# Cross-attention products on 32-row and 32-column tiles in a hybrid decoder layer

## The chip, the core and the metric

The kernel runs on one core of one Trainium2 chip. The metric is device time of one execution in microseconds (us), lower is better. Three executions of the kernel before took 487.26, 488.16 and 488.65 us; the median is 488.16 us.

## What is computed

One decoder layer with five branches that read the same input `x` (256 tokens, 1024 features): A and B are attentions with masks, C a forgetting attention, D a gated delta rule, E a cross-attention into 256 memory tokens. Each branch gives 384 features per token, which are gated by `silu(z)`, multiplied by the branch's output matrix and by a sigmoid of merge logits, and summed. An output matrix, a residual and a LayerNorm follow. The change is in branch E alone, four heads of 96 features:

```
k, v = split(mem_n @ w_kv, 2)
q = q.reshape(B, S, 4, 96) * 96 ** -0.5
p = softmax(einsum('bshd,bmhd->bhsm', q, k))
o_e = einsum('bhsm,bmhd->bshd', p, v).reshape(B, S, 384)
...
o = o * silu(z)
y = einsum('bsnc,ncd->bsnd', o, w_branch)
y = sum(sigmoid(merge_logits) * y, axis=2)
```

## The kernel before

All large products are made from float32 operands that are split in two parts, `hi` (ACT, L123) and `lo` (DVE, L124), and multiplied three times (`mm3`, L128: hi·hi, hi·lo, lo·hi). They are cut into units: a unit loads 128x1024 (or 128x384) weights by DMA, splits them, and multiplies them in two or three chunks. The list `ORDER` says in which order the units come; its end is `ze eq mk mv merge_d merge_b merge_e`. A `merge_x` block has eight pairs of units: 24 products of merge logits (`mm<-xhi,hi` and so on) and 9 products of the gated branch output with its output matrix (`mm<-f,hi`). Splits run one unit ahead (`SA`), in three buffers (`NHI`).

Everything small runs as side streams, Python generators of which up to three advance by one step after each chunk: attention of C, A and B (`attend`), the delta rule, the memory LayerNorm, and `cross`, which is branch E. Where a unit needs the output of a stream (`need("oge")` in `merge_e`), the streams are driven on until it is there. On top of that the framework's scheduler orders the instructions of each engine, so a line that is written next to another one need not run next to it. Each engine then takes its own instructions strictly in that order.

The matrices of PSUM are tiles of four kinds: three `mm` (the large products), one `lg` of two banks (logits), two `tp` (transposes), one `av` (values).

Branch E before: `evac_k` (L853) and `evac_ve` (L863) take keys and values out of PSUM. A head's 96 features lie across the three 128-row tiles of keys and queries, so `HQ` (L880) cuts the heads into one or two pieces of rows, six products for four heads. The last head is multiplied over all 128 rows, against a copy of the keys (`kp`) whose first 32 rows are zero. `cross` (L882) runs four chains, one for 128 tokens and two heads, two chains alive at a time (`LIVES[3]`): logits (L897), maximum on DVE (L900), exponential on ACT (L905), four transposes (L911), copy (L914), value products with tokens as rows (L920). After the second pair of heads the values are scaled by the reciprocal of the sums (L925). Then `token_gate` (L870) transposes the result back to features as rows (L875), multiplies it by the gate and splits it.

A product of two float32 operands that are not split (L897, L920, L135) leaves two records in the trace, that is two passes. A transpose leaves one.

Of the kernel before, what the change touches and what calls it, by code (L numbers as in the profile page):

```python
# [10 lines left out]
F32R = mybir.dt.float32r  # L11
AF = mybir.ActivationFunctionType
ALU = mybir.AluOpType
AX = mybir.AxisListType

P = 128
S = 256
D = 1024
KD = 8
BW = 384  # L20
H = 6
HD = 64
NB = 5
# [7 lines left out]
         " merge_c zb bq2 ze eq mk mv merge_d merge_b merge_e").split()  # L31
MERGES = [n for n in ORDER if n.startswith("merge")]
STREAMS = "base c levels solve b a gate_d cross norm".split()
LIVES = 2, 2, 1, 2

# [40 lines left out]
def kernel(ctx: ExitStack, tc: tile.TileContext, T: dict, out: bass.AP):  # L76
# [19 lines left out]
    def f3t(dt=F32, shape=(P, 3, S)):  # L96
        return f3.tile(list(shape), dt, tag="f3", name=nm("f3"))

    def spt(tag, shape, dt=F32, bufs=None):
        return sp.tile(list(shape), dt, tag=tag, name=nm(tag), bufs=bufs)  # L100
# [47 lines left out]
    R = {}  # L148
# [99 lines left out]
    def stepper(gens, n, force=False):  # L248


        k = 0
        for g in list(gens):
            if k == n:
                break
            if not force and ready.get(id(g), 0) > tick[0]:
                continue
            try:
                d = next(g)
                if d is not False:
# [593 lines left out]
    def evac_k(p, m, b):  # L853
        if m == 0:
            R["ke"] = f3t()
        A_.activation(R["ke"][:, m], p, AF.Copy)
        if m == 2:
            kp = R["kp"] = spt("kp", (P, S), bufs=1)
            V_.memset(kp[0:32], 0.0)
            V_.tensor_copy(kp[32:64], p[32:64])  # L860
            V_.tensor_copy(kp[64:128], p[64:128])

    def evac_ve(p, t):  # L863
        if t == 0:
# [5 lines left out]
    def token_gate(o, zs, br, scalar=None):  # L870
        dst = R["og" + br] = (f3t(F32R), f3t(F32R))
        for m in range(3):
            pt = tpps((P, S))
            for t in range(2):
                PE.transpose(pt[:, t * P:(t + 1) * P], o[:, t, m * P:(m + 1) * P], ident)  # L875
            yield
            yield from gate(pt, zs, m, dst, scalar)
        flag("og" + br)

    HQ = [[(0, 0, 96)], [(0, 96, 128), (1, 0, 64)], [(1, 64, 128), (2, 0, 32)], [(2, 0, 128)]]  # L880

    def cross():  # L882
        yield from wait("ze", "eq", "ve")
        ke, kp, qe, ve = R["ke"], R["kp"], R["eq"], R["ve"]
        oe = f3t(shape=(P, 2, BW))
        avt, smt = {}, {}

        def pair(t, g):
            if g == 0:
                smt[t] = spt("sme", (P, 4), bufs=2)  # L890
            lg = lgps()
            hs = (2 * g, 2 * g + 1)
            for x, h in enumerate(hs):
                parts = HQ[h]
                for i, (m, a0, a1) in enumerate(parts):
                    krhs = kp if (h == 3) else ke[:, m]
                    PE.matmul(lg[:, x, :S], qe[a0:a1, m, t * P:(t + 1) * P], krhs[a0:a1], start=i == 0, stop=i == len(parts) - 1)  # L897
            yield
            mxe = spt("mxe", (P, 2), bufs=3)
            V_.tensor_reduce(mxe, lg[:, :, :S], axis=AX.X, op=ALU.max, negate=True)  # L900
            yield
            pes = []
            for x, h in enumerate(hs):
                pe = spt("pr", (P, S), bufs=NPR)
                A_.activation(pe, lg[:, x, :S], AF.Exp, bias=mxe[:, x:x + 1], accum_out=smt[t][:, h:h + 1])  # L905
                pes.append(pe)
            yield
            p2 = tpps((P, 2, 2, P))
            for pe, pt in zip(pes, (p2[:, 0], p2[:, 1])):
                for x in range(2):  # L910
                    PE.transpose(pt[:, x], pe[:, x * P:(x + 1) * P], ident)  # L911
            yield
            pT = spt("pT", (P, 2, 2, P), bufs=2)
            A_.activation(pT, p2, AF.Copy)  # L914
            yield
            if g == 0:
                avt[t] = avps((P, 4, 96))
            for i, h in enumerate(hs):
                for x in range(2):
                    PE.matmul(avt[t][:, h], pT[:, i, x], ve[:, x, h * 96:(h + 1) * 96], start=x == 0, stop=x == 1)  # L920
            if g == 1:
                yield
                rse = spt("rse", (P, 4), bufs=2)
                V_.reciprocal(rse, smt[t])
                V_.tensor_tensor(oe[:, t].rearrange("p (h d) -> p h d", h=4), avt[t],  # L925
                                 rse[:, :, None].to_broadcast([P, 4, 96]), op=ALU.mult)

        todo = [pair(t, g) for t in range(2) for g in range(2)]
        live = []
        while todo or live:  # L930
            while todo and len(live) < LIVES[3]:
                live.append(todo.pop(0))
            stepper(live, LIVES[3])
            yield 1
        yield from token_gate(oe, R["ze"], "e")

    def d_gate():
        yield from wait("od", "zd")
# [176 lines left out]
def _layout(inp):  # L1115

    f = np.float32
    x = np.asarray(inp["x"], f)[0]
    w = np.asarray(inp["w_in"], f)[0]
    b = np.asarray(inp["b_in"], f)[0]  # L1120
    kv = np.asarray(inp["w_mem_kv"], f)[0]
    offs = np.cumsum([0, 1152, 2304, 384, 1152, 6, 1152, 6, 6, 384, 1920, 5120])
    oA, oBqk, oBv, oC, oCf, oD, oBeta, oDec, oE, oZ, oM = offs[:11]
    start = {"aq": oA, "ak": oA + 384, "av": oA + 768, "cq": oC, "ck": oC + 384, "cv": oC + 768,
             "dq": oD, "dk": oD + 384, "dv": oD + 768, "eq": oE, "bv": oBv}
    for g in range(3):
        start[f"bq{g}"] = oBqk + 384 * g
        start[f"bk{g}"] = oBqk + 1152 + 384 * g
    for n, i in BR.items():
        start["z" + n] = oZ + 384 * i  # L1130

    def cols(name):
        if name == "mk":
            return kv[:, 0:384]
        if name == "mv":
            return kv[:, 384:768]
        return w[:, start[name]:start[name] + 384]

    def fm(m):
        n = m.shape[1] // P  # L1140
        return m.reshape(KD, P, n, P).transpose(1, 2, 0, 3).reshape(P, n * 1024)

    r = {}
    r["xT"] = x.T.reshape(KD, P, S).transpose(1, 0, 2)
    r["x"] = x
    r["mem"] = np.asarray(inp["mem"], f)[0]
    r["wf"] = np.stack([fm(cols(n)) for n in FM])
    r["wt"] = np.stack([cols(n).reshape(KD, P, 384).transpose(1, 0, 2).reshape(P, 3072) for n in TM])
    wm = np.stack([fm(w[:, oM + 1024 * n:oM + 1024 * (n + 1)]) for n in range(NB)]).reshape(NB, P, KD, 1024)
    wb = np.asarray(inp["w_branch"], f)[0].reshape(NB, 3, P, KD, P).transpose(0, 2, 3, 1, 4).reshape(NB, P, KD, 384)  # L1150
    r["wm"], r["wb"] = wm.reshape(NB, P, KD * 1024), wb.reshape(NB, P, KD * 384)
    cs = [slice(start["cv"], start["cv"] + 384), slice(oCf, oCf + 6), slice(oDec, oDec + 6), slice(oBeta, oBeta + 6)]
    r["wcs"] = np.concatenate([w[:, s] for s in cs], 1).reshape(KD, P, 402).transpose(1, 0, 2).reshape(P, KD * 402)
    r["vcb"] = np.concatenate([b[s] for s in cs])[None]
    bc = [np.zeros(384, f) if n == "mk" else b[start[n]:start[n] + 384] for n in FM] + [b[oM:oM + 5120]]
    r["bcol"] = np.concatenate(bc).reshape(-1, P).T
    r["vb"] = np.stack([b[start[n]:start[n] + 384] for n in ("av", "bv")])[None]
    r["wo"] = np.asarray(inp["w_out"], f)[0].reshape(KD, P, D).transpose(1, 0, 2).reshape(P, 8192)
    r["convw"] = np.asarray(inp["conv_w"], f)[0].reshape(4, 9, P).transpose(2, 1, 0)
    r["adt"] = np.concatenate([np.asarray(inp["a_log"], f)[0], np.asarray(inp["dt_bias"], f)[0]])[None]  # L1160
    r["gnw"] = np.concatenate([np.asarray(inp["gdn_norm_w"], f)[0]] * 2)[:, None]
    r["mgb"] = np.stack([np.asarray(inp["mem_ln_g"], f).reshape(KD, P).T, np.asarray(inp["mem_ln_b"], f).reshape(KD, P).T], 1)
    r["lngb"] = np.stack([np.asarray(inp["ln_g"], f)[0], np.asarray(inp["ln_b"], f)[0]])[None]
    r["cst"] = _consts()
    return {k: np.ascontiguousarray(v) for k, v in r.items()}
# [16 lines left out]
```

## Time and profile before

| | |
|---|---|
| median of 3 runs | 488.16 us |
| profiled execution | 489.4 us |
| its span, first to last instruction | 487.6 us |
| mean granted clock of TensorE | 0.977 |
| PE busy | 469.8 us, 96% of the span |
| DVE busy | 336.1 us, 69% |
| ACT busy | 270.6 us, 55% |
| HBM read | 79.37 MB |

The table's span lies 1.8 us below the time of the same execution: the rest is before the first and after the last instruction. A matmul's recorded length contains its way through the array, so two that follow each other overlap in the record. What one costs on PE is therefore read from the distance between the starts of neighbours. "[0.89 <-ACT hi L123]" behind a row says that the engine was idle for 0.89 us and which result ended it.

### The profile page before, as it was taken

How to read it: one execution, taken by the hardware profiler on the slowest of the kernel's cores; microseconds unless marked ns; L12 is line 12 of the kernel's file. 1: busy time of each engine (PE TensorE's matmuls, PEld its weight loads, DVE VectorE, ACT ScalarE, POOL GpSimd, SP SyncE). 2: the span in 40 equal slices, each digit the busy share in tenths (PEclk: the TensorE clock that was granted, in tenths of full speed). 3: DMA queues.
4: the chain of work that ended last, by engine and by line, in shares of the span. 5: the costliest groups of instructions: out<-in, count | busy, mean ns of one | idle time of the engine just before them, and what ended most of it. 6: DMA issues, size and time to landing. Idle time of an engine off the chain costs nothing.

```text
span 487.6 us, 10147 instructions
## 1 busy us (share of the span) xinstructions
PE 469.8 (96%) x3957; PEld 439.2 (90%) x3957; DVE 336.1 (69%) x764; ACT 270.6 (55%) x521; POOL 30.5 (6%) x36
## 2 busy tenths in 40 slices
PE   7999999989989999999999999999999999999994
PEld 3999999979988999999999999988987899999973
DVE  4898998875983435568976665666667457678747
ACT  5546684763773333466854455846657445566610
POOL 0000040120000000000001210000012111100000
PEclk9999999989998699999999999999999999999997
DMA  8995667554444113245656786252753345577302
GB/s 263 367 369 169 202 202 250 161 144 121 146 105 116 44 60 114 84 140 174 204 155 209 222 260 215 78 167 77 279 191 120 104 125 173 182 231 235 131 1 86
DMA packets 35050, 81.38 MB, mean 167 GB/s; under 512 B 8969, under 2 KB 17467, under 8 KB 34875
## 3 DMA queue, kind: packets, MB, share of 16 engines
q1 hardware_dynamic: 34715, 80.22, 52.1%
q8 instruction: 31, 0.51, 0.4%
q10 hardware_dynamic: 288, 0.52, 0.3%
q14 instruction: 16, 0.13, 0.1%
HBM read 79.37 MB, written 1.36 MB: 166 GB/s over the span
## 4 chain that ended last, share of the span: by engine, by line
PE 84%; DVE 6%; DMA 4%; ACT 3%; issue 1%; SPq 1%; POOL 0%; DVEq 0%; POOLq 0%
PE mm L128 67%; PE lg L135 3%; PE lg L128 2%; DVE lo L124 2%; PE tp L128 2%; ACT pr L754 2%; PE av L135 2%; PE lg L897 1%; PE lg L773 1%; DMA raw<-in_wcs_dram 1%; ACT hi L123 1%; DVE pr L738 1%; DMA scr<-t 1%; PE av L920 1%; PE tp L632 1%
## 5 line engine op out<-in xcount | busy, mean ns | idle before, releaser
L124 DVE TENSOR_TENSOR lo<-raw,hi 128x1024 fp32r<-128x1024 f32 (+4 forms) x163 | 170.7, 1049 | 89.6 <-ACT hi L123 89.0
L128 PE MATMUL mm<-xhi,hi 128*128 128x256 f32 x776 | 221.3, 285 | 0.4 <-ACT hi L123 0.4
L123 ACT ACTIVATE hi<-raw 128x1024 fp32r<-128x1024 f32 (+4 forms) x163 | 146.4, 901 | 131.8 <-PE mm L128 90.2
L128 PE MATMUL mm<-xhi,lo 128*128 128x256 f32 x776 | 219.2, 283 | 0.3 <-DVE lo L124 0.3
L128 PE MATMUL mm<-xlo,hi 128*128 128x256 f32 x776 | 219.0, 282 | 0.0
L128 PEld LDWEIGHTS mm<-xhi,hi 128*128 128x128 f32 x776 | 148.1, 191 | 3.9 <-issue 2.0
L128 PEld LDWEIGHTS mm<-xhi,lo 128*128 128x128 f32 x776 | 147.9, 191 | 3.4 <-issue 1.6
L128 PEld LDWEIGHTS mm<-xlo,hi 128*128 128x128 f32 x776 | 148.2, 191 | 0.9 <-issue 0.7
L128 PE MATMUL mm<-f,hi 128*128 128x256 f32 x240 | 45.3, 283 | 0.4 <-ACT hi L123 0.4
L972 POOL TENSOR_TENSOR yacc<-yacc,yt 128x256 f32<-128x256 f32 x24 | 19.8, 824 | 303.3 <-DVE yt L971 294.1
L128 PEld LDWEIGHTS mm<-f,hi 128*128 128x128 f32 x240 | 36.7, 188 | 0.9 <-ACT hi L123 0.6
L128 PE MATMUL mm<-f,lo 128*128 128x256 f32 x120 | 33.9, 283 | 0.0
L128 PEld LDWEIGHTS mm<-f,lo 128*128 128x128 f32 x120 | 22.6, 188 | 0.1
L754 ACT ACTIVATE pr<-pr,mm 128x128 f32<-128x128 f32 (+1 forms) x36 | 15.9, 444 | 4.8 <-DVE mm L745 4.8
L954 ACT ACTIVATE th<-mm,bcol 128x256 f32<-128x256 f32 x40 | 18.4, 460 | 0.0
L128 PE MATMUL mm<-hi,xhi 128*128 128x384 f32 (+1 forms) x48 | 15.8, 353 | 2.0 <-ACT hi L123 2.0
L128 PE MATMUL mm<-lo,xhi 128*128 128x384 f32 (+1 forms) x48 | 16.8, 349 | 0.4 <-DVE lo L124 0.4
L135 PE MATMUL lg<-f,f 64*128 64x256 f32 (+1 forms) x144 | 16.9, 351 | 0.0
L738 DVE CUSTOM_DVE_ANT_0 pr<-lg,cst 128x128 f32<-128x128 f32 (+1 forms) x48 | 14.4, 352 | 3.6 <-PE lg L135 3.6
L971 DVE SCALAR_TENSOR_TENSOR yt<-th,mm 128x256 f32<-128x256 f32 x32 | 13.5, 420 | 4.7 <-PE mm L128 2.9
L128 PE MATMUL mm<-hi,xlo 128*128 128x384 f32 (+1 forms) x48 | 16.5, 345 | 0.0
L480 POOL TENSOR_SCALAR_AFFINE_SELECT pr<-pr 128x256 f32<-128x256 f32 x6 | 9.5, 1591 | 93.9 <-DVE pr L479 93.9
(234 smaller groups left out, 570.6 us busy)
## 6 DMA issues: line engine op xcount, KB each, us to landing
raw<-in_wf_dram SPq DMA_DIRECT2D x60, 512.0 KB, 4.5
raw<-in_wm_dram SPq DMA_DIRECT2D x40, 512.0 KB, 3.6
raw<-in_wb_dram SPq DMA_DIRECT2D x40, 192.0 KB, 2.4
raw<-in_wt_dram SPq DMA_DIRECT2D x12, 384.0 KB, 3.6
raw<-in_wo_dram SPq DMA_DIRECT2D x8, 512.0 KB, 5.9
gr<-gscr SPq DMA_DIRECT2D x12, 128.0 KB, 3.6
raw<-in_wcs_dram SPq DMA_DIRECT2D x3, 402.0 KB, 6.3
raw<-in_mem_dram SPq DMA_DIRECT2D x2, 512.0 KB, 3.2
```

The source lines that it names most:

```text
L123: A_.activation(hi, src, AF.Copy)
L124: V_.tensor_tensor(lo, src, hi.bitcast(F32), op=ALU.subtract)
L128: ins = PE.matmul(pt, l, r, start=start, stop=stop)
L135: PE.matmul(pt, l, r, start=start, stop=stop)
L480: G_.affine_select(E[:, 0::2], E[:, 0::2], pattern=[[0, 2], [1, P]], compare_op=ALU.is_ge, fill=-BIG, base=0, channel_multiplier=-1)
L632: PE.matmul(pt[r, x], Uc[r, 6 * t + h], V[r, t, h], start=True, stop=True)
L738: V_.tensor_tensor_reduce(l[:, sl], pts[x][:, sl], mk[x][:, sl], 1.0, 3.0e38, ALU.add, ALU.min, mx[x][:, t, g:g + 1])
L754: A_.activation(l[:, sl], l[:, sl], AF.Exp, bias=mms[x][:, t:t + 1], scale=-1.0, accum_out=sm_[x][:, t, g:g + 1])
L773: PE.transpose(lg[:, x, i * P:(i + 1) * P], L[x][0][:, i * P:(i + 1) * P], ident)
L954: A_.activation(th, p, AF.Tanh, bias=bcol[:, i:i + 1], scale=0.5)
L971: V_.scalar_tensor_tensor(yt, st_["th"], 1.0, st_["p"], op0=ALU.add, op1=ALU.mult)
L972: (V_ if last else G_).tensor_tensor(yacc[:, d], yacc[:, d], yt, op=ALU.add)
```

## The change

The columns of E's query, key and gate weights (and the rows of its output matrix) are permuted on the host, so that head `h` has rows 32h to 32h+31 of each of the three tiles. The masked copy `kp` is gone. `cross` runs one chain for 128 tokens and all four heads; the second chain starts when the first has made its transposes. `cross` now also waits for `ogb`, the end of branch B's attention.

```diff
-        if m == 2:
-            kp = R["kp"] = spt("kp", (P, S), bufs=1)
-            V_.memset(kp[0:32], 0.0)
-            V_.tensor_copy(kp[32:64], p[32:64])
-            V_.tensor_copy(kp[64:128], p[64:128])
...
     def cross():
-        yield from wait("ze", "eq", "ve")
+        yield from wait("ze", "eq", "ve", "ogb")
...
+        HE = [slice(32 * h, 32 * h + 32) for h in range(4)]
+        def tokens(t):
+            ts = slice(t * P, (t + 1) * P)
             lg = lgps()
-            for x, h in enumerate(hs):
-                for i, (m, a0, a1) in enumerate(HQ[h]):
-                    PE.matmul(lg[:, x, :S], qe[a0:a1, m, ts], krhs[a0:a1], ...)
+            pts = [lg[:, 0, :S], lg[:, 1, :S], tpps((P, S)), tpps((P, S))]
+            for m in range(3):
+                together(*[(pts[h], qe[r, m, ts], ke[r, m], m == 0, m == 2) for h, r in enumerate(HE)])
...
+            V_.reciprocal(rse, sme)
+            for h in range(4):
+                V_.tensor_scalar(pes[h], pes[h], rse[:, h:h + 1], None, op0=ALU.mult)
...
-                    PE.matmul(avt[t][:, h], pT[:, i, x], ve[:, x, h * 96:(h + 1) * 96], ...)
+            av = avps((P, 3, P))
+            for m in range(3):
+                for x in range(2):
+                    together(*[(av[r, m], ve[:, x, 96 * h + 32 * m:96 * h + 32 * m + 32], pTs[h // 2][:, h % 2, x], x == 0, x == 1)
+                               for h, r in enumerate(HE)])
+            V_.tensor_tensor(g, av, zs[:, :, ts], op=ALU.mult)
+            split(dst[0][:, :, ts], dst[1][:, :, ts], g)
...
-        yield from token_gate(oe, R["ze"], "e")
```

`together` (L132) issues its products one behind the other and nothing more. The logits are now 24 products of 32 rows, the values 48 products of 32 columns; the six transposes back and the scaling of the values are gone, and the probabilities are scaled instead, eight times.

How the instructions stand: first PE inside the block `mv`, before its last unit (`mm<-hi,big` are products of the memory, `f` the queries and keys of E, `lg_4426` the transposes of branch B). Before:

```order
L128 MATMUL mm_4453<-hi_4475,big_3186 128x384
L128 MATMUL mm_4453<-lo_4476,big_3186 128x384
L128 MATMUL mm_4453<-hi_4475,big_3187 128x384
L128 MATMUL mm_4452<-hi_4510,big_3186 128x384
L128 MATMUL mm_4453<-hi_4510,big_3186 128x384
L773 MATMUL lg_4426<-cst,pr_4245 128x128 x3
```

Now:

```order
L128 MATMUL mm_4449<-lo_4472,big_3186 128x384
L128 MATMUL mm_4449<-hi_4471,big_3187 128x384
L135 MATMUL tp_4776<-f_734_4347,f_705_4199 128x256
L135 MATMUL tp_4775<-f_734_4347,f_705_4199 128x256
L135 MATMUL tp_4776<-f_734_4347,f_705_4199 128x256
L128 MATMUL mm_4448<-hi_4506,big_3186 128x384
L128 MATMUL mm_4449<-hi_4506,big_3186 128x384
L773 MATMUL lg_4426<-cst,pr_4245 128x128 x3
```

Three of the first chain's logit products, of heads 2 and 3, stand directly ahead of the last unit of `mv`, and three more (`tp_4775`, `tp_4776`, `tp_4775`) stand ten products earlier; the two other heads (`lg_4774`, six products) follow much later, behind the last pair of B.

Second, PE in `merge_d`, from the unit that follows B's last twelve exponentials on. Before (B's exponentials are not shown, they are ACT's):

```order
L128 MATMUL mm_4984<-f_470_2951,hi_4935 128x256
L128 MATMUL mm_4984<-f_469_2950,lo_4936 128x256
L911 MATMUL tp_4660<-cst,pr_4631 128x128 x2
L897 MATMUL lg_4599<-f_734_4347,f_705_4199 128x256 x2
L897 MATMUL lg_4599<-kp_4442,f_705_4199 128x256
L911 MATMUL tp_4660<-cst,pr_4633 128x128 x2
L128 MATMUL mm_5040<-f_469_2950,hi_5001 128x256
L128 MATMUL mm_5040<-f_470_2951,hi_5001 128x256
L128 MATMUL mm_5005<-xhi,lo_4981 128x256
```

Now:

```order
L128 MATMUL mm_4961<-f_470_2951,hi_4865 128x256
L128 MATMUL mm_4961<-f_469_2950,lo_4866 128x256
L773 MATMUL lg_4682<-cst,pr_4501 128x128 x3
L128 MATMUL mm_5039<-f_469_2950,hi_4982 128x256
L128 MATMUL mm_5039<-f_470_2951,hi_4982 128x256
L128 MATMUL mm_4986<-xhi,lo_4958 128x256
```

E's products and transposes have left this place, and the three that stood 18 products ahead of it (`lg_4595`, L897) too. B's own six transposes (L773), which came later before, stand here instead.

Third, PE in `merge_d` at the second chain of E (all of it new):

```order
L128 MATMUL mm_5143<-xlo,hi_5120 128x256
L135 MATMUL tp_4902<-f_734_4347,f_705_4199 128x256 x3
L128 MATMUL mm_5143<-xhi,lo_5121 128x256
L128 MATMUL mm_5143<-xhi,hi_5120 128x256
L135 MATMUL tp_4903<-f_734_4347,f_705_4199 128x256 x3
L909 MATMUL lg_4879<-cst,pr_4823 128x128 x2
...
L135 MATMUL av_4922<-pT_4897,f_778_4568 32x128 x2
L128 MATMUL mm_5176<-f_470_2951,hi_5139 128x256
L135 MATMUL lg_4901<-f_734_4347,f_705_4199 128x256 x6
L135 MATMUL av_4922<-pT_4899,f_778_4568 32x128 x2
L135 MATMUL av_4922<-pT_4897,f_778_4568 32x128 x2
```

Head 2 and head 3 of the second chain stand alone, three products each, with large products between them; heads 0 and 1 (`lg_4901`) come later, in the middle of the first chain's values. The values are written in the order of the heads, two products first, then 22 in one row.

## Rows read from the trace of the kernel before

**Rows 1.** The page: busy us of each engine, share of the span, instructions.

```profile
PE 469.8 (96%) x3957; PEld 439.2 (90%) x3957; DVE 336.1 (69%) x764; ACT 270.6 (55%) x521; POOL 30.5 (6%) x36
```

**Rows 2.** Groups by line: shapes xcount | busy us, mean ns | idle before.

```profile
L897 PE MATMUL lg<-f,f 32*128 32x256 f32 (+2 forms) x20 | 6.4, 419 | 0.0
...
L897 PE MATMUL lg<-kp,f 128*128 128x256 f32 x4 | 1.4, 431 | 0.0
...
L920 PE MATMUL av<-f,pT 128*128 128x96 f32 x32 | 4.1, 271 | 0.0
...
L767 DVE TENSOR_SCALAR pr<-pr,rs 128x128 f32<-128x128 f32 (+1 forms) x36 | 10.2, 327 | 0.2
```

**Rows 3.** Timeline of PE, one logit block: start us, length, instruction [idle before].

```profile
364.49 0.28 PE L128 MATMUL mm<-xhi,lo 128*128 128x256 f32 x1
364.61 1.85 PE L897 MATMUL lg<-f,f 96*128 96x256 f32 x6
...
366.60 0.29 PE L128 MATMUL mm<-xlo,hi 128*128 128x256 f32 x1
...
364.82 0.38 PE L897 MATMUL lg<-f,f 96*128 96x256 f32 x1
```

**Rows 4.** Timeline of PE, one block of value products.

```profile
376.49 0.28 PE L128 MATMUL mm<-f,hi 128*128 128x256 f32 x1
376.61 1.03 PE L920 MATMUL av<-f,pT 128*128 128x96 f32 x8
...
377.62 0.28 PE L128 MATMUL mm<-f,lo 128*128 128x256 f32 x1
```

**Rows 5.** Timeline of PE, one pair of transposes.

```profile
403.46 0.28 PE L128 MATMUL mm<-xhi,hi 128*128 128x256 f32 x1
403.58 0.38 PE L875 MATMUL tp<-cst,f 128*128 128x128 f32 x2
...
403.91 0.28 PE L128 MATMUL mm<-xhi,lo 128*128 128x256 f32 x1
```

**Rows 6.** Timeline of PE, branch B's logits: two heads, 64 rows each.

```profile
332.16 0.28 PE L128 MATMUL mm<-big,lo 128*128 128x256 f32 x1
332.37 0.93 PE L135 MATMUL lg<-f,f 64*128 64x128 f32 x8
...
333.56 0.28 PE L128 MATMUL mm<-big,lo 128*128 128x256 f32 x1
```

**Rows 7.** Timeline of PE, branch B's values: two heads, 64 columns each.

```profile
386.60 0.28 PE L128 MATMUL mm<-xlo,hi 128*128 128x256 f32 x1
386.80 0.87 PE L135 MATMUL av<-pT,f 128*64 128x256 f32 x8
...
387.83 0.28 PE L128 MATMUL mm<-xhi,hi 128*128 128x256 f32 x1
```

**Rows 8.** Timeline of PE, ahead of the last unit of `mv`.

```profile
340.11 0.34 PE L128 MATMUL mm<-hi,big 128*128 128x384 f32 x1
341.35 0.62 PE L128 MATMUL mm<-hi,big 128*128 128x384 f32 x2 [0.89 <-ACT hi L123]
```

**Rows 9.** Timeline of PE, then ACT and DVE, after branch B's last logits.

```profile
368.43 0.28 PE L128 MATMUL mm<-xhi,lo 128*128 128x256 f32 x1
369.06 0.50 PE L128 MATMUL mm<-f,hi 128*128 128x256 f32 x2 [0.36 <-ACT hi L123]
370.01 0.39 PE L128 MATMUL mm<-xhi,hi 128*128 128x256 f32 x1 [0.45 <-ACT hi L123]
...
373.77 0.29 PE L128 MATMUL mm<-xhi,lo 128*128 128x256 f32 x1
...
362.87 0.40 ACT L754 ACTIVATE pr<-pr,mm 128x128 f32<-128x128 f32 x1 [2.69 <-DVE mm L745]
...
371.09 1.22 DVE L124 TENSOR_TENSOR lo<-raw,hi 128x1024 fp32r<-128x1024 f32 x1
```

**Rows 10.** Windows: PE, PEld, DVE, ACT, POOL busy (x), granted clock, DMA.

```profile
162.00:171.00 9.00, 9.00 (x92) 8.44 (x90) 2.75 (x7) 2.21 (x3) 0.00 (x0) 0.50 0.18 57
360.00:400.00 40.00, 39.20 (x295) 34.20 (x296) 23.05 (x50) 23.74 (x65) 6.18 (x7) 1.00 0.36 113
```

More of the change, by code (lines that the diff above doesn't have):

```diff
@@ L33 @@
 STREAMS = "base c levels solve b a gate_d cross norm".split()
-LIVES = 2, 2, 1, 2
+LIVES = 2, 2, 1
 SIDE, GAP, LD, SA, NRAW, NHI = 3, 1, 4, 1, 7, 3
@@ L878, in token_gate @@
         flag("og" + br)
-    HQ = [[(0, 0, 96)], [(0, 96, 128), (1, 0, 64)], [(1, 64, 128), (2, 0, 32)], [(2, 0, 128)]]
     def cross():
-        yield from wait("ze", "eq", "ve")
[L884 to L890, printed above, removed]
-            lg = lgps()
-            hs = (2 * g, 2 * g + 1)
-            for x, h in enumerate(hs):
[L894 to L897, printed above, removed]
+        yield from wait("ze", "eq", "ve", "ogb")
@@ L898, in pair @@
+        ke, qe, ve, zs = R["ke"], R["eq"], R["ve"], R["ze"]
+        dst = R["oge"] = (f3t(F32R), f3t(F32R))
+        HE = [slice(32 * h, 32 * h + 32) for h in range(4)]
+        def tokens(t):
+            ts = slice(t * P, (t + 1) * P)
+            lg = lgps()
+            pts = [lg[:, 0, :S], lg[:, 1, :S], tpps((P, S)), tpps((P, S))]
+            for m in range(3):
+                together(*[(pts[h], qe[r, m, ts], ke[r, m], m == 0, m == 2) for h, r in enumerate(HE)])
             yield
-            mxe = spt("mxe", (P, 2), bufs=3)
@@ L900, in pair @@
-            V_.tensor_reduce(mxe, lg[:, :, :S], axis=AX.X, op=ALU.max, negate=True)
+            mxe, sme, rse = [spt(n, (P, 4), bufs=2) for n in ("mxe", "sme", "rse")]
+            V_.tensor_reduce(mxe[:, 0:2], lg[:, :, :S], axis=AX.X, op=ALU.max, negate=True)
+            for h in (2, 3):
+                V_.tensor_reduce(mxe[:, h:h + 1], pts[h], axis=AX.X, op=ALU.max, negate=True)
             yield
             pes = []
-            for x, h in enumerate(hs):
+            for h in range(4):
@@ L904, in pair @@
                 pe = spt("pr", (P, S), bufs=NPR)
-                A_.activation(pe, lg[:, x, :S], AF.Exp, bias=mxe[:, x:x + 1], accum_out=smt[t][:, h:h + 1])
+                A_.activation(pe, pts[h], AF.Exp, bias=mxe[:, h:h + 1], accum_out=sme[:, h:h + 1])
                 pes.append(pe)
+                if h % 2:
+                    yield
+            V_.reciprocal(rse, sme)
+            for h in range(4):
+                V_.tensor_scalar(pes[h], pes[h], rse[:, h:h + 1], None, op0=ALU.mult)
@@ L907, in pair @@
             yield
-            p2 = tpps((P, 2, 2, P))
-            for pe, pt in zip(pes, (p2[:, 0], p2[:, 1])):
+            p2 = lgps().rearrange("p g (h x c) -> p g h x c", h=2, x=2)
+            for h in range(4):
                 for x in range(2):
-                    PE.transpose(pt[:, x], pe[:, x * P:(x + 1) * P], ident)
+                    PE.transpose(p2[:, h // 2, h % 2, x], pes[h][:, x * P:(x + 1) * P], ident)
+            flag("pe")
             yield
-            pT = spt("pT", (P, 2, 2, P), bufs=2)
@@ L914, in pair @@
-            A_.activation(pT, p2, AF.Copy)
+            pTs = []
+            for g in range(2):
+                pT = spt("pT", (P, 2, 2, P), bufs=2)
+                A_.activation(pT, p2[:, g], AF.Copy)
+                pTs.append(pT)
             yield
-            if g == 0:
-                avt[t] = avps((P, 4, 96))
-            for i, h in enumerate(hs):
+            av = avps((P, 3, P))
+            for m in range(3):
                 for x in range(2):
-                    PE.matmul(avt[t][:, h], pT[:, i, x], ve[:, x, h * 96:(h + 1) * 96], start=x == 0, stop=x == 1)
@@ L921, in pair @@
[L921 to L933, printed above, removed]
+                    together(*[(av[r, m], ve[:, x, 96 * h + 32 * m:96 * h + 32 * m + 32], pTs[h // 2][:, h % 2, x], x == 0, x == 1)
+                               for h, r in enumerate(HE)])
@@ L934, in cross @@
+            yield
+            g = spt("pr", (P, 3, P), bufs=NPR)
+            V_.tensor_tensor(g, av, zs[:, :, ts], op=ALU.mult)
+            yield
+            split(dst[0][:, :, ts], dst[1][:, :, ts], g)
+        live, todo = [tokens(0)], [tokens(1)]
+        while live:
+            stepper(live, 2)
+            if todo and "pe" in done:
+                live += todo
+                todo = []
             yield 1
-        yield from token_gate(oe, R["ze"], "e")
+        flag("oge")
     def d_gate():
@@ L1130, in _layout, with bias @@
         start["z" + n] = oZ + 384 * i
+    pe = np.arange(384).reshape(4, 3, 32).transpose(1, 0, 2).reshape(384)
     def cols(name):
         if name == "mk":
-            return kv[:, 0:384]
+            return kv[:, 0:384][:, pe]
         if name == "mv":
             return kv[:, 384:768]
-        return w[:, start[name]:start[name] + 384]
+        m = w[:, start[name]:start[name] + 384]
+        return m[:, pe] if name in ("eq", "ze") else m
+    def bias(name):
+        v = b[start[name]:start[name] + 384]
+        return v[pe] if name in ("eq", "ze") else v
     def fm(m):
@@ L1149, in _layout @@
     wm = np.stack([fm(w[:, oM + 1024 * n:oM + 1024 * (n + 1)]) for n in range(NB)]).reshape(NB, P, KD, 1024)
-    wb = np.asarray(inp["w_branch"], f)[0].reshape(NB, 3, P, KD, P).transpose(0, 2, 3, 1, 4).reshape(NB, P, KD, 384)
+    wb = np.asarray(inp["w_branch"], f)[0].copy()
+    wb[BR["e"]] = wb[BR["e"]][pe]
+    wb = wb.reshape(NB, 3, P, KD, P).transpose(0, 2, 3, 1, 4).reshape(NB, P, KD, 384)
     r["wm"], r["wb"] = wm.reshape(NB, P, KD * 1024), wb.reshape(NB, P, KD * 384)
@@ L1154, in _layout @@
     r["vcb"] = np.concatenate([b[s] for s in cs])[None]
-    bc = [np.zeros(384, f) if n == "mk" else b[start[n]:start[n] + 384] for n in FM] + [b[oM:oM + 5120]]
+    bc = [np.zeros(384, f) if n == "mk" else bias(n) for n in FM] + [b[oM:oM + 5120]]
     r["bcol"] = np.concatenate(bc).reshape(-1, P).T
```

## The prediction

> **What bounds the kernel.** The page's first part comes first: PE is busy for 96% of the span, DVE for 69%, ACT for 55% [rows 1]. So a change of this size counts by what it does to PE: how long PE works for branch E, and how long PE stands still. The second view is the groups by line, which give the number of E's records: 24 for the logits (12 products of two passes) and 32 for the values [rows 2]. Their mean lengths overlap and are no price. The price comes from the timeline of PE, from the distance between the starts of the large products around a block. The reader is to see there that one large product of 256 columns takes 0.12 us from start to start (364.49 to 364.61 [rows 3]), and that a block costs more than its products, since the first start after it comes late too. The third view is the same timeline at the places where PE idles: it names ACT's `hi` as what ended the wait. Whatever E does there instead of waiting is free.
>
> **E's work on PE before.** From the large product before the logit block to the second one after it are 366.60 − 364.49 = 2.11 us; less two products of 0.12, the block of three products costs 1.87 us [rows 3]. A value block costs 377.62 − 376.49 − 0.24 = 0.89 [rows 4], two transposes 403.91 − 403.46 − 0.24 = 0.21 [rows 5]. E has four logit blocks, four value blocks, 16 + 6 transposes: 4 × 1.87 + 4 × 0.89 + 11 × 0.21 = 13.4 us.
>
> **E's work on PE after.** One pass over 256 columns takes 364.82 − 364.61 = 0.21 us, here on 96 rows [rows 3]; I take the same for 32. Branch B shows two tiles side by side: its logit block has, for each of two heads, two passes of 256 columns and two of 128. By columns that is 3 × 0.21 = 0.63 if the heads overlap and 1.26 if not; the block costs 333.56 − 332.16 − 3 × 0.12 = 1.04 [rows 6]. So they overlap, and 0.41 is the fixed price of leaving the full array and coming back. Its value block, on two column tiles, gives 387.83 − 386.60 − 0.24 = 0.99, a fixed price of 0.36 [rows 7].
>
> The diff writes four heads in turn, but the order of PE keeps that only in part. Logits, first chain: heads 2 and 3 come as two pieces of three products; each piece is two products deep, 4 × 0.21 + 0.41 = 1.25. Heads 0 and 1 alternate, three deep: 6 × 0.21 + 0.41 = 1.67. Second chain: head 2 alone 1.67, head 3 alone 1.67, heads 0 and 1 together 1.67. Sum 2 × 1.25 + 4 × 1.67 = 9.2 us, against 7.5 before: twice the products, and most of the four-way overlap lost.
>
> Values, for each chain: two products apart, then 22 in one row. I take passes of 128 columns at half of 0.21, and all four column tiles side by side, though the trace shows only two: 0.21 + 0.36 = 0.57, and 6 products deep, 12 × 0.105 + 0.36 = 1.62; 4.4 us for both chains, against 3.6. The bounds: two at a time, as rows 7 show it, makes the long piece 11 deep, 2.2 us more in all; one at a time 22 deep, 6.7 us more. I take the four, as nothing in those rows shows the second tile costing anything. The Trainium skill (TensorE: Matmul & The Clock Gate, Measured speedup vs the span model) gives less than full overlap, 3.07 for four row tiles and 2.38 for three column tiles of 512 columns; rows 6 and 7 show no such loss for two tiles. Taken for four column tiles, 3.07 would make the two long pieces an estimated 0.8 us longer in all.
>
> Transposes: 16 remain, 8 × 0.21 = 1.7; the six back are gone. Sum after 9.2 + 4.4 + 1.7 = 15.3, that is **+1.9 us** on PE. It could be 1 us less if neighbouring pieces share a switch.
>
> **The first wait.** Ahead of the last unit of `mv` PE stands from 340.11 to 341.35 for ACT's `hi` [rows 8], less about one and a half slots of 0.12 for a product of 384 columns: 1.06 us. Two pieces of the first chain's logits (2.5 us) now stand before that place. ACT is held there by B's exponentials, on which E has no hand, so the wait goes: **−1.06**. Bounds: 0 if those pieces themselves wait for keys, −1.06 if not; the third key tile has left ACT before the exponentials by its order, so I take −1.06.
>
> **The second wait.** After B's last logits, ACT starts twelve exponentials at 362.87, as soon as DVE's maximum is there; then come the splits. PE waits for `hi` at 369.06 and 370.01, and DVE's `lo` of the next 128x1024 weights ends at 371.09 + 1.22 = 372.31 [rows 9]. PE cannot take up the long run of products before that. Before, E filled this time: a logit block (1.87) and a block with two pairs of transposes (1.87 + 0.42), 4.16 us; PE took up the long run at 373.77. E no longer has anything there. PE then comes 4.16 us earlier to a `lo` that is only 373.77 − 372.31 = 1.46 us earlier, and 2.7 us turn into waiting. B's six transposes, which came later before, fall into it, 3 × 0.21 = 0.6. Loss of cover: **+2.1**. The bounds are 0, if ACT and DVE get done as much sooner, and 2.7.
>
> **What costs nothing.** DVE gets eight scalings of at most 0.33 [rows 2], 2.6 us, and loses the copies of `kp`, the scaling and some of the gate; ACT keeps eight exponentials and four copies. Between 360 and 400 us DVE is busy for 23.05 and ACT for 23.74 of 40 [rows 10]; splits run a unit ahead, and E's result is wanted only by `merge_e`, which starts some 200 products after E's last one in the order. On the path the scalings would cost those 2.6. The wait for `ogb` delays the first chain behind B's last pair; queued behind it are only E's own steps and, on ACT and DVE, splits that have a unit's time to spare. The order of SP's loads changes by one place, POOL's not at all. The start and, from the third pair of units of `merge_b` on, the end are the same on every engine.
>
> **Sum.** +1.9 − 1.06 + 2.1 = +2.9 us. Against the profiled execution's 489.4 that is 492.3; its median of 488.16 lies 1.2 lower, so for a median I forecast **491.1 us**. A measurement of this kernel can tell about 0.3%, 1.5 us, from no change.
>
> **Rivals.**
> - The cover isn't lost: PE, ACT and DVE get past B's last pair sooner because E's first exponentials and maximum no longer stand in their queues there. For it: DVE's maximum of E and two of ACT's exponentials did stand in this stretch. Against it: the chain starts at 362.87 with B's own maximum and ends with B's own scalings, and E's work came behind or in DVE's gaps. It decides if `lo` is ready 2 us earlier. Then +0.8: 489.0, not slower by what can be told. Chance 0.17.
> - The values do not run four at a time: +2.9 + 2.2 = 5.1 by two, +9.6 by one, 493.3 to 497.8. For it: no row here shows more than two tiles. Against it: the second tile is free in rows 7. Chance 0.12.
> - The logits do run four in turn, as the diff writes it: two blocks of 1.67 instead of 9.2, −5.9 on PE, −3.0 in all: 485.2, faster. PE's order speaks against it, as large products and tens of us lie between the heads. Another gain on PE of that size (no price for the switch between small tiles, 8 pieces × 0.4 = 3.2) would do the same. Chance 0.08. The same section of the Trainium skill (TensorE: Matmul & The Clock Gate) measures four row tiles together, which is this case.
> - The clock falls in the stretches of small tiles. From 162 to 171 us, among the delta rule's small products, the granted clock was 0.50 with PE busy throughout [rows 10], a loss of half of 9 us: +2.9 + 4.5, 495.6. Against it: with E and B's narrow products before, 360 to 400 shows 1.00. Chance 0.04.
>
> **The numbers.** The forecast itself has 0.59. Its own range, from the bounds above (1 us of shared switches, part of the cover kept, some of the values' overlap lost), is 489.3 to 493.5. To the other cases: 487.3 leaves out the third rival and a little more, 495.0 the clock and the values one by one; about 0.2 is outside. Slower by over 0.3%: most of the forecast (0.50), the values and the clock, 0.12 + 0.04, together 0.66. Within: the cover kept and the low end of the forecast, 0.23. Faster: the third rival and a rest, 0.11.
>
> **What would show it.** Right: the logit pieces of 32 rows cost 1.6 to 1.7 each where three products stand in a row; four value products start within a few ns of each other; no wait of 1 us near 341, and one or two waits for `hi` and `lo` of 2 to 3 us in all near 369 to 374, ended by ACT and DVE; PE's work for E near 15 us; the distance to the end the same from the third unit of `merge_b` on. Wrong: the waits near 370 not longer than before, new waits at the second chain's transposes or values, or a lower clock there.

## The result and the profile after

| | before | after |
|---|---|---|
| median on the chip of the prediction's comparison, 4 runs each | 487.74 us | 493.31 us (491.13 to 494.26) |
| ratio, 95% interval | | 1.0109 (1.0074 to 1.0143) |
| profiled execution, its span | 489.4, 487.6 us | 492.68, 490.6 us |
| PE busy | 469.8 us | 473.5 us |

The change makes the kernel slower by about 5.6 us, 1.1%. Two more comparisons of the unedited change, on other occasions, gave 494.93 against 488.40 (1.0118, 1.0073 to 1.0163) and 492.29 against 487.41 (1.0081, 1.0048 to 1.0114), so 4.9 to 6.5 us.

Runs of one kernel lie as far apart as this effect is large, and they go with the mean granted clock that each run lists. Over all 104 runs of before and 17 of after in this study the mean of that clock is 0.981 and 0.974. Among runs at 0.976 to 0.9785 the medians are 489.4 (37 runs) and 492.3 (3), at 0.979 to 0.9815 they are 487.9 (31) and 491.3 (2). Medians below are over all runs of a kernel; the ratios leave out the slow runs, those over 1.5% above the fastest of their kernel, which takes 4 of 12 runs from e1 (the other eight have a median of 487.98) and 5 of 11 from e2 (490.44), out of this ordinary scatter.

To compare profiles without the early part, I use one distance: from the start of branch B's last block of eight logit products ahead of `mv` to the end of the span. Up to there PE's order is the same in both kernels. For the kernel before the distance is 487.6 − 332.37 = 155.2 us [rows 6].

First the page of after, PE's row and the granted clock over 40 slices of 12.3 us:

```profile
PE 473.5 (97%) x4039; PEld 443.1 (90%) x4039; DVE 337.7 (69%) x767; ACT 270.1 (55%) x520; POOL 32.2 (7%) x36
...
PEclk9999999999997899999999999999998899999997
```

Beside the dip at slices 13 and 14, which the kernel before has too [rows 10], there is one at slices 31 and 32, where E runs. The windows of after split that stretch (columns: span, PE busy and records, granted clock, DMA share, GB/s):

```profile
366.00:369.00 3.00, 0.90 (x8) 1.00 0.00 0
369.00:372.40 3.40, 3.24 (x15) 0.50 0.30 63
372.40:386.00 13.60, 13.60 (x104) 1.00 0.57 181
386.00:389.50 3.50, 3.50 (x17) 0.51 0.25 69
389.50:406.00 16.50, 16.50 (x203) 1.00 0.34 94
```

Twice the clock is at the lower of its two levels, 1.2 GHz (the 0.50 of these rows; 1.00 is 2.4 GHz), for about 3.4 us: behind a stretch in which PE worked for 0.90 of 3 us, and again at 386 with PE busy throughout. Before, the clock was 1.00 there [rows 10].

The timeline of PE of after, at the places that the prediction named:

```profile
331.58 0.93 PE L135 MATMUL lg<-f,f 64*128 64x128 f32 x8
...
337.24 0.69 PE L128 MATMUL mm<-hi,big 128*128 128x384 f32 x3
337.86 1.13 PE L135 MATMUL tp<-f,f 32*128 32x256 f32 x6
...
339.20 0.34 PE L128 MATMUL mm<-hi,big 128*128 128x384 f32 x1
...
340.61 0.34 PE L128 MATMUL mm<-hi,big 128*128 128x384 f32 x1
340.88 1.13 PE L135 MATMUL tp<-f,f 32*128 32x256 f32 x6
341.93 0.45 PE L128 MATMUL mm<-hi,big 128*128 128x384 f32 x1
...
359.92 0.93 PE L135 MATMUL lg<-f,f 64*128 64x128 f32 x8
...
366.62 0.28 PE L128 MATMUL mm<-xhi,lo 128*128 128x256 f32 x1
369.16 0.79 PE L128 MATMUL mm<-f,hi 128*128 128x256 f32 x2 [2.26 <-ACT hi L123]
...
372.94 0.28 PE L128 MATMUL mm<-xhi,lo 128*128 128x256 f32 x1
...
382.67 0.28 PE L128 MATMUL mm<-xlo,hi 128*128 128x256 f32 x1
382.88 1.56 PE L135 MATMUL tp<-f,f 32*128 32x256 f32 x6
...
384.59 0.28 PE L128 MATMUL mm<-xhi,hi 128*128 128x256 f32 x1
...
404.55 0.39 PE L128 MATMUL mm<-f,hi 128*128 128x256 f32 x1
404.86 1.50 PE L135 MATMUL av<-pT,f 128*32 128x128 f32 x44
...
406.52 0.28 PE L128 MATMUL mm<-xhi,hi 128*128 128x256 f32 x1
```

The wait of 0.89 us ahead of the last unit of `mv` [rows 8] is gone: PE runs on at 340.88 with a piece of E's logits and takes up `mm<-hi,big` at 341.93 with no idle time. The waits of 0.36 and 0.45 us [rows 9] have become one of 2.26. A piece of one head, three products deep, moves the first to the second large product around it from 382.67 to 384.59, that is 1.69 us after two slots of 0.115. The long piece of values costs 406.52 − 404.55 − 0.23 = 1.74. The distance to the end is 490.6 − 331.58 = 159.0 us, 3.8 more than before. Another 0.3 us lie outside the span, in every run: time less span is 1.83 for before and 2.1 for after.

### The profile page after: what moved, and what is told of

Read it like the earlier page. It is cut to its first block, busy times and chain, and to the rows that moved or that the text cites. A ratio compares the mean times of both kernels' runs of the same rounds, so it can differ in the third digit from the quotient of the medians.

```text
span 490.6 us, 10305 instructions
## 1 busy us (share of the span) xinstructions
PE 473.5 (97%) x4039; PEld 443.1 (90%) x4039; DVE 337.7 (69%) x767; ACT 270.1 (55%) x520; POOL 32.2 (7%) x36
## 5 line engine op out<-in xcount | busy, mean ns | idle before, releaser
L973 POOL TENSOR_TENSOR yacc<-yacc,yt 128x256 f32<-128x256 f32 x24 | 21.6, 900 | 302.6 <-DVE yt L972 293.4
L135 PE MATMUL lg<-f,f 64*128 64x256 f32 (+2 forms) x168 | 20.1, 357 | 0.0
L128 PE MATMUL mm<-hi,xhi 128*128 128x384 f32 (+1 forms) x48 | 17.4, 389 | 0.9 <-ACT hi L123 0.9
L128 PE MATMUL mm<-lo,xhi 128*128 128x384 f32 (+1 forms) x48 | 18.0, 375 | 0.0
L128 PE MATMUL mm<-hi,xlo 128*128 128x384 f32 (+1 forms) x48 | 17.9, 373 | 0.0
L972 DVE SCALAR_TENSOR_TENSOR yt<-th,mm 128x256 f32<-128x256 f32 x32 | 13.4, 419 | 3.0 <-PE mm L128 2.1
```

The source lines that it names most:

```text
L128: ins = PE.matmul(pt, l, r, start=start, stop=stop)
L135: PE.matmul(pt, l, r, start=start, stop=stop)
L972: V_.scalar_tensor_tensor(yt, st_["th"], 1.0, st_["p"], op0=ALU.add, op1=ALU.mult)
L973: (V_ if last else G_).tensor_tensor(yacc[:, d], yacc[:, d], yt, op=ALU.add)
```

## The experiments

Theory: E's products cost more on PE because PE's order cut the logits into pieces, its cover over the wait near 367 is lost, and the granted clock falls where PE stands or runs small pieces. Rivals stand with each.

**e1, the logits four in turn.**

```diff
-                together(*[(pts[h], qe[r, m, ts], ke[r, m], m == 0, m == 2) for h, r in enumerate(HE)])
+                for h, r in enumerate(HE):
+                    tc.keep_in_program_order(PE.matmul(pts[h], qe[r, m, ts], ke[r, m], start=m == 0, stop=m == 2))
```

> The changed kernel with the 12 logit products of each chain held together on PE, so that four heads run in turn. All of the result is kept. My theory (small tiles next to each other overlap, and the pieces that PE's order cut out of the logits are what makes E long there): each chain's logits are one block of about 1.7 us in place of 4.6 (9.2 to 3.4 us in all), the wait of 1.06 us near 341 comes back, since nothing of E stands before that place any more, the idle time of 2.3 us near 367 to 369 stays with the half clock behind it, and the half clock near 386 to 389 goes, since no piece of one head is left there: about 5 to 7 us less than the changed kernel, 486 to 488. Rival (E's work on PE isn't what costs; the time is lost on DVE and ACT or by the early falls of the clock): 0 to 2 us less, 491 to 493.

Median 488.71 us (12 runs), within the scatter of before (488.09, 34 runs). Timeline of PE, the first passes of one block, the two waits, and the windows behind the second:

```profile
376.35 0.48 PE L889 MATMUL lg<-f,f 32*128 32x256 f32 x2
376.36 0.48 PE L889 MATMUL tp<-f,f 32*128 32x256 f32 x2
376.67 0.38 PE L889 MATMUL lg<-f,f 32*128 32x256 f32 x2
...
340.58 0.62 PE L128 MATMUL mm<-hi,big 128*128 128x384 f32 x2 [0.90 <-ACT hi L123]
...
368.31 0.51 PE L128 MATMUL mm<-f,hi 128*128 128x256 f32 x2 [2.26 <-ACT hi L123]
...
369.20:372.60 3.40, 3.34 (x15) 0.50 0.46 154
372.60:406.00 33.40, 33.37 (x368) 1.00 0.46 136
```

Four row tiles run side by side, each chain's logits cost 1.5 us more than the block they join, and the first wait is back, as expected. The half clock at 369 is there, that at 386 is not. The distance is 485.6 − 331.61 = 154.0, 5.0 less than after. The theory holds, down to the wait that comes back and the fall that goes; the time is 3.6 to 6.2 less than the three medians of after, which were taken on other occasions, and lies just above the 486 to 488 that were named.

**e2, E without the wait for branch B's gate.**

```diff
-        yield from wait("ze", "eq", "ve", "ogb")
+        yield from wait("ze", "eq", "ve")
```

> The changed kernel without the wait for branch B's gate ahead of E, so that E's first chain falls again into the time after B's last logits. All of the result is kept. My theory (lost cover): PE's idle time of 2.3 us near 367 and the fall of the granted clock behind it, at 369, go: 2 to 4 us less than the changed kernel, 489 to 491. Rival (the cover isn't worth anything, since DVE and ACT do E's work later at the same cost): within 1 us of the changed kernel, 492 to 494, with a wait of the same length at another place.

Median 491.85 (11 runs), distance 490.8 − 332.75 = 158.0. The long wait became three of 0.48, 0.44 and 0.50, but in the one profile taken, of an execution of 492.88 us, the clock did not stay up: from 373.3 it was 0.50 for 6.8 us, over two one-head pieces that this order puts there. The 2 to 4 us that the theory promised did not come, and the reason is not the rival's: the wait did shrink.

**e3, both edits.** The diffs of e1 and e2 together.

> The two edits together: no wait for branch B's gate, and each chain's 12 logit products held together on PE. All of the result is kept. If their effects add: 7 to 10 us less than the changed kernel, 483 to 486, faster than the kernel before. If the block of 1.7 us is too short a cover for the wait near 367, about 2 us of it stay: 485 to 488.

Median 488.26 (12 runs), distance 485.9 − 330.86 = 155.0. The sum of effects did not come: E's block stands at 363, ahead of the wait, and its maxima (1.1 us on DVE) come ahead of the `lo` of the next large weights there. PE waits 0.48 us for `hi`, then 0.70 and 1.19 for `lo`, and the clock falls at 371.3. The block was too short a cover, as the second guess had it.

**e4, the wait for B's gate put into the kernel before.**

```diff
-        yield from wait("ze", "eq", "ve")
+        yield from wait("ze", "eq", "ve", "ogb")
```

> The kernel before, with one edit: E's step waits for branch B's gate, as in the changed kernel; layout and products of E are those of before. All of the result is kept. My theory: the loss of the cover alone is 2 to 3.5 us, 490 to 491, with PE idle for about 2 us near 367 to 369; if the idle time itself lets the granted clock fall there, a fall to 0.50 follows at about 369 although no small tiles are near. Rival (only the products of 32 rows cost): within 1 us of the kernel before.

Median 490.80 (12 runs), ratio 1.0059 (1.0034 to 1.0084). Wait and windows:

```profile
367.96 0.51 PE L128 MATMUL mm<-f,hi 128*128 128x256 f32 x2 [2.26 <-ACT hi L123]
...
360.00:368.80 8.80, 6.53 (x55) 1.00 0.17 63
368.80:372.20 3.40, 3.29 (x15) 0.50 0.51 153
372.20:406.00 33.80, 33.80 (x255) 1.00 0.40 120
```

This one line alone costs 2.7 us by the medians and 2.8 by the distance (489.2 − 331.25 = 158.0). The wait has the length of after's, and the fall of the clock follows it without any of the change's products of 32 rows, while one at 386 does not come. So the first fall goes with the wait and does not need the change's small tiles. The wait does not always bring it: in e9 it came without a fall.

**e5, the change again, beside the next three.** No edit.

> The changed kernel itself, unedited, again, so that it stands beside the next three on one chip. Both theories: 492 to 494 us, with the granted clock at 0.50 for 3.4 us at about 369 and again at about 386, and PE idle for 2.3 us ahead of the first.

Median 494.93 (6 runs). Half clock from 375.0 and from 392.1, distance 496.3 − 337.06 = 159.2, as the theory said; its early part was the slowest of all profiles, and the median lies above the 492 to 494 that were named.

**e6, PE's wait filled with zeros.** In `chunk` of `merge_branch`:

```diff
                 p = st_["p"] = mmps()
+                if br == "d" and d == 4:
+                    for _ in range(20):
+                        PE.matmul(p, zero[:, 0:P], zero[:, :256], start=True, stop=True)
```

> The changed kernel with 20 products of zeros (bf16, 128 x 256, some 0.11 us each, 2.2 us in all) on PE just ahead of the product that waits near 367, into the tile that this product then overwrites; the result is the same. PE idles there anyway for 2.3 us, so the fillers cost nothing themselves. My theory (it is PE standing still that lets the granted clock fall at 369, and the one-head pieces of 32 rows that let it fall at 386): the first fall goes, the second stays, 0.5 to 1.7 us less than the changed kernel run beside it. Rival (the 32-row products are behind both falls, or both come at fixed times): both falls stay and the time is the same or up to 0.5 us more.

Median 491.15 (12 runs), distance 489.6 − 332.95 = 156.7. The fillers, a block of one-head pieces and transposes, and the window over all of E:

```profile
370.11 2.34 PE L965 MATMUL mm<-zero 128*128 128x256 bf16 x20 [1.84 <-ACT th L955]
372.21 0.49 PE L128 MATMUL mm<-f,hi 128*128 128x256 f32 x2
...
385.27 1.56 PE L135 MATMUL tp<-f,f 32*128 32x256 f32 x10
386.76 0.44 PE L909 MATMUL lg<-cst,pr 128*128 128x128 f32 x2
387.12 0.69 PE L135 MATMUL tp<-f,f 32*128 32x256 f32 x2
387.75 0.88 PE L909 MATMUL lg<-cst,pr 128*128 128x128 f32 x6
...
331.00:470.00 139.00, 137.16 (x1160) 1.00 0.51 161
```

The fillers did not start in the idle time: their tile was itself waited for, `th` of ACT, which stands behind B's exponentials like `hi`. So they came after a wait of 1.84 us and took another 2.10 (370.11 to 372.21). Still the median is 3.8 us under e5's and the distance 1.8 to 2.5 under after's, and neither fall came. That the second stayed away too was not expected: here the two one-head pieces stand in one block with the transposes, not apart with large products between. Which of the two, the other order or the other history of the clock, is behind it stays open. What e6 gains lies there, in E's second chain: from B's last logits to the long run of products it takes 13.2 us, after takes 13.0. And since the first fall stayed away in e9 without any fillers, this profile does not show that they kept it away.

**e7, e1 and e6 together.**

> The changed kernel with the logits held together for four heads in turn, and the 20 products of zeros in PE's wait near 367. The result is the same. My theory: neither fall of the clock is left after 300 us, and 0.5 to 1.7 us less than the kernel with the logits held together alone (488.7): 487 to 488.2, within 0.3% of the kernel before or a little faster. Rival: no less than 488.7.

Median 488.73 (12 runs), distance 486.5 − 332.50 = 154.0: no fall after 180 us, and not faster than e1. The fillers cost as much as the fall does. The rival was right.

**e8, four in turn in the second chain alone.** The diff of e1 under `if t == 1`.

> The changed kernel with the logits held together in the second chain alone; the first chain's stay as PE's order cuts them, two pieces of them ahead of the last unit of the memory's values. The result is the same. My theory: the fall near 386 goes (its one-head pieces belonged to the second chain), the one near 369 stays, the wait of 0.9 us near 340 stays gone; the second chain's logits cost about 1.7 in place of 5.0 us: 4 to 5 us less than the changed kernel run beside it, 488.5 to 489.5. Rival (the fall near 386 comes from the value blocks or the transposes): it stays, and 2.5 to 3.5 us less.

Median 488.66 (12 runs), distance 489.7 − 335.38 = 154.3, 4.7 less than after and 4.9 less than e5. Windows:

```profile
373.40:376.80 3.40, 3.40 (x17) 0.50 0.47 139
376.80:410.00 33.20, 33.20 (x357) 1.00 0.47 140
```

The wait near 340 stays gone, that of 2.26 stays with 3.4 us of half clock behind it, and from 376.8 to 410 the clock is 1.00. The second fall belongs to the second chain as PE's order cuts it.

**e9, the change a third time.** No edit.

> The changed kernel, unedited, a third time, because the two measurements so far differ (493.3 and 494.9) and the place of the early falls of the clock, before 180 us, varies from run to run. From the start of branch B's first eight logit products in a row to the end the profiles give 159.0 and 159.2 us, against 155.2 for the kernel before. My theory: 159.0 to 159.3 again, with one fall at the end of the wait for hi and one some 17 us later, and a median of 492 to 494. Rival (the falls in E's stretch come at random, as the early ones do): one of them missing or elsewhere, the distance 157 to 158.

Median 492.29 (7 runs), distance 491.2 − 332.69 = 158.5. Timeline and windows:

```profile
361.04 0.93 PE L135 MATMUL lg<-f,f 64*128 64x128 f32 x8
...
370.27 0.51 PE L128 MATMUL mm<-f,hi 128*128 128x256 f32 x2 [2.26 <-ACT hi L123]
...
373.55 0.39 PE L128 MATMUL mm<-xhi,lo 128*128 128x256 f32 x1 [0.41 <-DVE lo L124]
...
366.00:376.00 10.00, 7.22 (x58) 1.00 0.30 83
...
386.90:390.30 3.40, 3.40 (x16) 0.50 0.19 60
```

Here the wait of 2.26 us brought no fall, and the kernel gained only 0.5 us by it (373.55 − 332.69 = 40.9 to where the long run is taken up, against 372.94 − 331.58 = 41.4): PE then waits 0.41 us for `lo` instead. The fall at 386.9 came. The distance lies between theory and rival.

**e10, the diffs of e8 and e2 together.**

> The changed kernel with the logits held together in the second chain alone and without the wait for branch B's gate: the first chain's two early pieces stand ahead of the last unit of the memory's values, its third piece ahead of the wait near 367, and the second chain runs four heads in turn. The result is the same. If the gains add: no wait of 0.9 near 340, 1.4 us of waits near 370 in place of 2.3, the second chain's logits 1.7 in place of 4 to 5, and no fall of the clock: from branch B's first eight logit products in a row to the end 152 to 153 us (155.2 before), 485 to 486.5, faster than the kernel before. If the three short waits let the clock fall as the long one does: 154 to 155, 487 to 488.

Median 488.44 (12 runs; before beside it 487.41), distance 487.4 − 332.79 = 154.6:

```profile
370.37 0.50 PE L128 MATMUL mm<-f,hi 128*128 128x256 f32 x2 [0.49 <-ACT hi L123]
371.31 0.39 PE L128 MATMUL mm<-xhi,hi 128*128 128x256 f32 x1 [0.44 <-ACT hi L123]
372.33 0.39 PE L128 MATMUL mm<-f,lo 128*128 128x256 f32 x1 [0.51 <-DVE lo L124]
...
373.50:376.90 3.40, 3.38 (x16) 0.50 0.80 261
```

Three short waits were followed by a fall of the clock as the long one is, and the four gains did not add up. No version of this study beats the kernel before by what can be measured.

**e11 and e12, weights split two units ahead**, in e1 and in the kernel before:

```diff
-SIDE, GAP, LD, SA, NRAW, NHI = 3, 1, 4, 1, 7, 3
+SIDE, GAP, LD, SA, NRAW, NHI = 3, 1, 4, 2, 7, 3
```

> The changed kernel with the logits held together for four heads in turn, and with the weights split two units ahead of the products in place of one (the tiles for it are there), so that a unit's hi stands ahead of branch B's exponentials in ACT's queue. The result is the same. My theory (PE waits at 340 and at 367 because hi stands behind the exponentials): both waits shrink to under 1 us in all and no fall of the clock comes after 180 us; 2 to 3.5 us less than with the logits held together alone (488.7): 485 to 486.5, faster than both kernels. Rival (the tile of partial sums, not hi, is what the product waits for, or splits that come earlier wait for loads or buffers elsewhere): the waits stay or move, 488 to 491.

> The kernel before with the weights split two units ahead, so that what the earlier split gives by itself is known. The result is the same. My theory: its two waits of 0.9 and 0.8 us go and nothing else changes: 486 to 487. Rival: new waits for loads or buffers, 488 to 491.

Medians 489.36 and 489.67 (12 runs each; before 488.33). The waits did not go, they moved. Timeline of PE and windows of e11:

```profile
343.88 0.33 PE L773 MATMUL lg<-cst,pr 128*128 128x128 f32 x1 [2.09 <-DVE pr L767]
...
372.23 0.33 PE L773 MATMUL lg<-cst,pr 128*128 128x128 f32 x1 [2.13 <-DVE pr L767]
...
345.50:348.90 3.40, 3.40 (x17) 0.50 1.02 419
372.80:376.20 3.40, 3.40 (x16) 0.50 0.34 73
```

With `hi` done earlier, PE's order brings B's transposes to this place, and they wait for B's own probabilities, which DVE scales (L767) after ACT's exponentials. Both waits are followed by a fall of the clock. e12 has 2.21 us of such a wait at 341.87 and half clock from 342.0. Both rivals were right that waits move and in the time; the loads and buffers that they named were not what PE then waited for.

## Why the prediction was right in direction and low in size

The measured median of 493.31 lies 0.2 us below the upper end of the stated range, 493.5; of the two later medians of the same kernel one, 494.93, lies above it. E's own work and the lost cover came as worked out. The falls of the clock were left out, two savings were not foreseen, and part of the loss lies where no term looked; that all this together stayed inside the range is in part luck.

Sum and distance, term by term. A block's cost is worked out as in the prediction, from the starts of the large products around it.

| term | predicted | measured |
|---|---|---|
| E on PE, before | 13.4 | 13.5 |
| E on PE, after | 15.3 | 15.4 (estimate for a clock of 1.00; 16.8 as it ran) |
| difference | +1.9 | +1.9 |
| first wait | −1.06 | −1.6 |
| lost cover | +2.1 | +2.1 (e9, without a fall there) |
| half clock at 369 | left out | +0.5 |
| half clock near 386 | left out | +1.7 (estimate, half of 3.4) |
| large products after the long run's start | 0 | −0.8 |
| sum | +2.9 | +3.8 (distance: +3.8) |

- **E's work before.** All its blocks add up to 13.5 us, as the few prices said.
- **The pieces.** The first two pieces cost 1.26 each by large products of 384 columns (337.24 + 2 × 0.174 to 339.20, less two slots of 0.174), predicted 1.25; a one-head piece 1.69, predicted 1.67; heads 0 and 1 cost 1.5 in each chain, predicted 1.67, because they join a block of values and share its switch; the values 1.74 and 0.64 for a chain, predicted 1.62 and 0.57. With 1.8 for the transposes the sum is 15.4. Two blocks of it ran in part at half clock (2.31 and 1.62 us); they are put here at the 1.92 (1.69 + 0.23) and 0.67 that like blocks of after cost at a clock of 1.00. In e6, where heads 2 and 3 of the second chain share one block with the transposes, E takes 14.6.
- **Four column tiles.** 44 passes take 1.50 us from the first start to the last end. Two at a time they would take 22 × 0.105 = 2.3, so they do run four at a time, and the rival that they don't falls. The Trainium skill (TensorE: Matmul & The Clock Gate, Measured speedup vs the span model) gives 3.07 for four row tiles of 512 columns. The 1.74 here lies 0.1 above full overlap as predicted; taken for these column tiles, 3.07 would make the piece an estimated 0.4 us longer than predicted, so the row stands nearer to full overlap.
- **The first wait** went, and its size was too low. From B's block ahead of `mv` to the start of B's last logits it is 359.83 − 332.37 = 27.46 us in the kernel before (the last logits are the row below) and 359.92 − 331.58 = 28.34 in after; less the two pieces, 2.52, after has 25.82, which is 1.6 less. The prediction took the recorded idle time alone; in before the next products behind that wait start late too. e1 brought the wait back (0.90) by taking the two pieces away.

```profile
359.83 0.93 PE L135 MATMUL lg<-f,f 64*128 64x128 f32 x8
```

- **The second wait.** From B's last logits to the long run of products it is 373.77 − 359.83 = 13.94 before [rows 9]; less E's two blocks, 4.21, 9.7 remain. In e9, where the clock did not fall, it is 373.55 − 361.04 = 12.51; less B's transposes, 0.68 (0.34 for three at a clock of 1.00, in e6), 11.8 remain: +2.1, as predicted. In after it is 13.02, +2.6 with the fall. PE stands 2.26 in one piece, in the range of 2 to 3 that was named. e4 shows that the one line that waits for `ogb` does this, with nothing else of the change.
- **The clock.** This is the step that failed. The prediction gave a falling clock 0.04, since 360 to 400 us of before shows 1.00 with narrow products [rows 10]. It argued from the kind of the products, although the same rows show 0.50 from 162 to 171 us with PE busy throughout; and in before PE never stood longer than 0.45 us between 360 and 400, where after stands 2.26. After has half clock behind the wait and again in the second chain. The first is worth 0.5 us (after against e9), because PE would else wait for `lo`. The second has no cover, as PE is busy throughout, and half of 3.4 us is 1.7; six transposes cost 1.62 in it and 0.67 at 399.64, with a clock of 1.00. Together 2.2 us, not the rival's 4.5. The first fall comes with the wait, without the change's small tiles too (e4); the second one does come among small tiles, as the rival had it.
- **The large products.** From the start of the long run to the end, less E and B's transposes, it is 103.8 us before and 103.0 in e6, where the clock does not fall; the 743 large products there are the same. No term foresaw these 0.8, and their cause is open.
- **What stays open.** The distance gives 3.8 us, with 0.3 outside the span 4.1, and the medians 4.9 to 6.5. By the distance, the rest lies ahead of B's block, where PE's order is the same. From 100 to 180 us the granted clock was 0.94, 0.87 and 0.91 in the three profiles of after and 0.89 in that of before, so it varies by itself; whether 17 runs only met worse early clocks, or the change has a part in it, isn't settled. That it has is suggested by the other versions with the change's layout and the same order there: e1, e2, e3, e6, e7, e8 and e10 lose 0.1 to 1.5 us more by their medians than by the distance and the 0.3, e4, with the layout of before, nothing.

What the cut logits cost can be read from e1: holding them together alone takes 5.5 us from E's work (15.4 to 9.9), brings the first wait back, +1.6, and removes the second fall, −1.7: −5.6 by these terms. By the distance it is −5.0; the 0.6 between lies behind B's last logits (13.3 us to the long run, 13.0 in after) and in the large products (103.3, 103.0 in e6).

## What to carry to other kernels

Products that are written to run side by side do so only if they are neighbours in the engine's final order; read that order, and pin the group if it has to hold. When work is moved away from a wait, price the wait twice: the idle time, and the clock that may be granted afterwards. In e11 and e12 a wait behind another engine's queue wasn't removed by having one of its results earlier: PE waited for the next result instead, 2.09 to 2.21 us.

## What was not expected of the hardware

PE stood still for 2.09 to 2.26 us in nine waits (after, e1, e4, e5, e8, e9, e12, and twice in e11). In eight of them the granted clock was at 0.50 within 1.7 us of the end of the wait, for 3.4 us; in e9 it stayed at 1.00. It stayed there in e6 and e7 too, where PE stood for 1.84 us and then ran the products of zeros. There is one profile for each of these versions. The kernel before, with waits of 0.89, 0.36 and 0.45, shows no such fall between 180 and 470 us. Three waits of 0.44 to 0.51 within 3 us (e10) were followed by the same fall as one long one. In all three profiles of the change the clock also fell in a stretch of one-head pieces and transposes, in after with PE busy for all of the 13.6 us before. What is needed for that is not settled: e6 ran the same products in one block at a clock of 1.00.
